# RMS norms of a decoder layer: the constant in a padded column, and one small step on another engine

## The chip, the cores and the metric

The kernel runs on one core of a Trainium2 chip, as one launch. The metric is the device time of that launch in microseconds (us). Instruction streams of five engines run side by side and meet only at semaphores: TensorE (PE, with its weight loads PEld), VectorE (DVE), ScalarE (ACT), GpSimd (POOL) and SyncE (SP, here used to issue DMAs). Each engine takes its own instructions in order.

## What is computed

One layer of a decoder over 1024 rows (tokens) of 1024 columns, in float32. With the sizes of this case (`DEPTH = 1`) the mixer is the pooling one:

```python
def rms_norm(x, g):
    xf = x.astype(jnp.float32)
    y = xf * lax.rsqrt(jnp.mean(xf * xf, axis=-1, keepdims=True) + EPS)
    return (y * g.astype(jnp.float32)).astype(x.dtype)
...
    h = rms_norm(x, norm_mix_g[layer])
    y = pool_mixer(h, pool_w[j], pool_b[j], pool_scale[j])
    x = x + y.astype(x.dtype)
    f = conv_ffn(rms_norm(x, norm_ffn_g[layer]), ffn_w_in[layer], ...)
    x = x + f.astype(x.dtype)
```

`pool_mixer` takes causal window means of 2, 4, 8 and 16 rows in four groups of columns, subtracts the row itself and multiplies each group by a 256x256 matrix. `conv_ffn` multiplies by a 1024x5632 matrix, convolves over three rows, gates with silu and multiplies by a 2816x1024 matrix. Nearly all the arithmetic lies in these last two products.

## The kernel before, in words

**Stages.** The 1024 rows are eight tiles of 128 rows, x0 to x7. In the first stage (to about 65 us of the profile) each tile goes through the mixer: its norm "a" (Square with a sum over the row on ACT, then a square root, then the factor on DVE), a band matrix scaled by that factor (`bandr`, `mixer_norm`), window sums by PE (`psd`), a copy to SBUF by ACT (`dh`), the 256x256 products and the bias by PE (`psy`), and the residual sum by DVE, which overwrites the tile (`mixer_out`, L267). Then follow the second norm "b", its application (`n2`, `ffn_norm`, L279), and eight transposes by PE (`pst`, `ffn_operand`). The rows that a window needs from the tile before come from a ninth tile, `x_edge`, whose own norm "e" scales `edge_band`, and whose window sums are `ps_edges`. In the second stage the 1024x5632 product runs by a Strassen-like scheme of seven products on operands that are each split in two (high part copied by ACT, L76 or L313; remainder by DVE, L77 or L314): banks X, Y, Z, L374. The third stage is the 2816x1024 product (L731), built likewise.

**The norm's arithmetic.** With m the sum of squares plus D*EPS and s the square root of m, one over s is wanted, but s comes from a table and is a little off. The kernel forms q = s*s + m and uses s divided by q (a factor two is folded into the weights). `rstd_of` (L154 to L163) issues, for each norm: on ACT Square with a sum (L157, one ACTIVATE and one read of the accumulator) and Sqrt with the constant as bias (L158); on DVE an addition of the constant to the sum (L159), s*s + m (L161) and a reciprocal (L162). There are 17 of them: a0 to a7, e, b0 to b7.

**What sets the order.** A scheduler lays each engine's instructions out by data dependences and by the hints `issue_after`, which hold an instruction back in the order until another has been placed. The tiles x2 to x6 lie in the pool `pre`, x0, x1 and x7 in the ring of seven buffers `hl` that later holds the split operands. SP's queue carries in order the loads of x, the stores of the new x (L268), the loads of the first weights (L322) and of one block of them (`S3`, L341). POOL's queue adds weight blocks to each other by accumulating DMAs (L336); their results are the operands S1, S2 and S4 of the second product.

Of the kernel before, what the change touches and what calls it, by code (L numbers as in the profile page):

```python
# [7 lines left out]
F32 = mybir.dt.float32  # L8
F32R = mybir.dt.float32r
BF16 = mybir.dt.bfloat16  # L10
AF = mybir.ActivationFunctionType
ALU = mybir.AluOpType
PSUM = bass.MemoryType.PSUM

P = 128
S = 1024
D = 1024
# [8 lines left out]
EPS = 1e-6  # L26
# [15 lines left out]
XBUFS = 5  # L42
# [6 lines left out]
def trunk_kernel(ctx: ExitStack, tc: tile.TileContext, x, consts, par, rows, pool_w, w_in, w_out, out):  # L49
    nc = tc.nc  # L50
# [6 lines left out]
    hls = ctx.enter_context(tc.tile_pool(name="hls", bufs=1))  # L57
# [4 lines left out]
    pp = pre.enter_context(tc.tile_pool(name="pre", bufs=1))  # L62
# [17 lines left out]
        return t  # L80


    xs = {}

    def load_x(j):
        if j < 2 or j >= 2 + XBUFS:
            xs[j] = hls.tile([P, D], F32, tag="hl", name=f"x{j}", bufs=7)
        else:
            xs[j] = pp.tile([P, D], F32, tag="x", name=f"x{j}", bufs=XBUFS)
        nc.sync.dma_start(xs[j], x[j * P : (j + 1) * P, :])  # L90

    cst = pp.tile([P, BD], F32, tag="cst", name="cst")
# [7 lines left out]
    scale = rows_raw[:, 0, :GRP]  # L100
# [33 lines left out]

    keep_warm(7)
    load_x(0)
    nc.sync.dma_start(cst[:, :E0], consts[:, :E0])
    load_x(1)
    nc.sync.dma_start(par_sb[:, GM:], par[:, GM:])
    nc.sync.dma_start(cst[:, E0:], consts[:, E0:])  # L140
    for g in range(0, NG, 2):
        nc.sync.dma_start(wp_raw[:, 2 * g : 2 * g + 4, :], pool_w[g : g + 2].rearrange("g (k p) d -> p (g k) d", p=P))
    load_x(2)

    nc.sync.dma_start(x_edge, x.rearrange("(j r) d -> r j d", r=P)[P - HALO :, :, :])
# [4 lines left out]
    ident = cst[:, ID:]  # L150

    marks = {}

    def rstd_of(src, name):  # L154
        junk = pp.tile([P, D], BF16, tag="junk", name=f"junk_{name}")
        st = pp.tile([P, 4], F32, tag="st", name=f"st_{name}", bufs=8)
        nc.scalar.activation(junk, src, AF.Square, accum_out=st[:, 0:1])  # L157
        marks[name] = nc.scalar.activation(st[:, 1:2], st[:, 0:1], AF.Sqrt, bias=eps_t).ins  # L158
        nc.vector.tensor_scalar(st[:, 0:1], st[:, 0:1], D * EPS, None, op0=ALU.add)  # L159

        nc.vector.scalar_tensor_tensor(st[:, 3:4], st[:, 1:2], st[:, 1:2], st[:, 0:1], op0=ALU.mult, op1=ALU.add)  # L161
        nc.vector.reciprocal(st[:, 2:3], st[:, 3:4])  # L162
        return st[:, 1:2], st[:, 2:3]  # L163
# [4 lines left out]
    bands, stats = {}, {}  # L168
# [84 lines left out]
    n2s = {}  # L253
    x1_dram = dram.tile([S, D], F32, tag="x1_dram", name="x1_dram")

    def mixer_out(j, stats=True):
        dh = ds.pop(j)
        ps = bank2(f"psy{j}")
        for c in range(NK):
            o = ps[:, c // 2 * GRP : (c // 2 + 1) * GRP]  # L260
            nc.tensor.matmul(o, dh[:, c, :], wps[:, c, :], start=c % 4 == 0, stop=False, skip_group_check=True)  # L261
        for h in range(2):
            cols = slice(h * NH, (h + 1) * NH)
            m = nc.tensor.matmul(ps[:, cols], ones, bias_hl[:, cols], start=False, stop=True, skip_group_check=True)  # L264
        marks[f"psy{j}"] = m.ins
        x1 = n2s[j] = xs.pop(j)
        marks[j] = nc.vector.tensor_tensor(x1, ps, x1, ALU.add).ins  # L267
        nc.sync.dma_start(x1_dram[j * P : (j + 1) * P, :], x1)  # L268
        if stats:
            mixer_out_stats(j)  # L270

    def mixer_out_stats(j):
        n2s[j] = (n2s[j], rstd_of(n2s[j], f"b{j}"))

    def ffn_norm(j):
        x1, r = n2s[j]
# [177 lines left out]

    def stat(j):
        if j in xs and j not in stats:
            stats[j] = rstd_of(xs[j], f"a{j}")

    scale_b = scale_rows()
    stat(0)  # L460
    mixer_norm(0)
    with tc.issue_after(marks["band0"]):
        nc.vector.tensor_tensor(b8, b8, rows8[:, 0, :], ALU.mult)
        stat(1)
# [12 lines left out]
    with tc.issue_after(marks["gain"]), tc.issue_after(marks["wps"]):  # L477
        stat(2)
        mixer_norm(2)
# [14 lines left out]
    with tc.issue_after(marks["band3"]), tc.issue_after(marks["edges"]):  # L494
        mixer_out_stats(0)
# [66 lines left out]
    def take(name):  # L562
# [15 lines left out]
    src = {  # L578
        "A11": lambda f: g_dram[f][:, s0], "A21": lambda f: g_dram[f][:, s1],
        "A12": lambda f: g_dram[f + NP2][:, s0], "A22": lambda f: g_dram[f + NP2][:, s1],  # L580
        "B11": lambda f: w_out[f * P : (f + 1) * P, s0], "B12": lambda f: w_out[f * P : (f + 1) * P, s1],
        "B21": lambda f: w_out[(f + NP2) * P : (f + NP2 + 1) * P, s0],
        "B22": lambda f: w_out[(f + NP2) * P : (f + NP2 + 1) * P, s1],
    }
# [91 lines left out]
    for k in range(-SLOOK, len(oevents)):  # L676
        p, f = oevents[k + SLOOK] if k + SLOOK < len(oevents) else (None, 0)
# [8 lines left out]
        with tc.issue_after(lasts[-1]) if lasts else nullcontext():  # L686
# [12 lines left out]
            p, f = oevents[k]  # L699
# [9 lines left out]
        if f == 0 and opens:  # L709
            for i in range(4):  # L710
                tag = ("XXYY" if set_ == "X" else "YZZZ")[i]
# [14 lines left out]
        for i, g, c, bank in steps:  # L726
            a, b = oops[p, g]
# [88 lines left out]
```

## Time and profile before

| | |
|---|---|
| time of the runs before, us | 701.71, 700.93, 700.96 (median 700.96) |
| profiled execution: span from first to last instruction, us | 699.1 |
| busy in that span | PE 692.5, PEld 575.8, DVE 597.9, ACT 343.0, POOL 13.3 us |
| granted TensorE clock | 1.000 |

The profile is of one execution, of which the span is known and not a time of its own; the timed runs are 1.8 to 2.6 us above that span. A row of the timeline gives start, duration, engine, source line, operation, output and input with their shapes, and in brackets how long the engine had been idle before and what ended that. A row of the chain of waits gives start, length and work of one piece of the path that ended last. A busy PE is not PE at its peak: matmuls overlap, and recorded ends lie some 0.2 us late.

### The profile page before, as it was taken

To read this page: it belongs to the slowest core of one execution; us is meant where nothing else is said; L and a number is where in the kernel's file an instruction comes from. 1 tells how busy PE (TensorE), PEld (TensorE's weight loads), DVE (VectorE), ACT (ScalarE), POOL (GpSimd) and SP (SyncE) were. 2 spreads that over 40 slices of the span, in tenths; PEclk is the share of its full clock that TensorE was granted. 3 is DMA by queue.
4 is the path that set the end of the run, shared out by engine and by line. 5 is a ranking of instruction groups with operands and counts; after the bars stand their busy time and mean duration, and the time that the engine had idled before them with its cause. 6 is when DMAs were issued, how large, how long until landed. Compare 5 with 4: busy or idle time off the path is not lost.

```text
span 699.1 us, 8512 instructions
## 1 busy us (share of the span) xinstructions
PE 692.5 (99%) x3164; PEld 575.8 (82%) x3164; DVE 597.9 (86%) x883; ACT 343.0 (49%) x515; POOL 13.3 (2%) x33
## 2 busy tenths in 40 slices
PE   9999999999999999999999999999999999999998
PEld 7898778888888888888888888888888888888886
DVE  4798999999888888888888888876887988999985
ACT  6686645554454454444454444444454344444431
POOL 3020000000000000000000000000000000000000
PEclk9999999999999999999999999999999999999999
DMA  8964112322212112222222212229989700122231
GB/s 279 304 170 121 61 60 91 120 91 91 90 64 89 68 57 86 91 91 90 91 90 91 91 69 82 97 87 350 326 301 339 269 22 0 61 90 89 63 106 61
DMA packets 32562, 85.49 MB, mean 122 GB/s; under 512 B 3692, under 2 KB 5384, under 8 KB 29704
## 3 DMA queue, kind: packets, MB, share of 16 engines
q1 hardware_dynamic: 31328, 82.83, 33.3%
q0 software_dynamic: 1184, 2.11, 1.7%
q8 instruction: 25, 0.41, 0.2%
q14 instruction: 17, 0.14, 0.1%
q10 hardware_dynamic: 8, 0.00, 0.0%
HBM read 62.89 MB, written 19.92 MB: 118 GB/s over the span
## 4 chain that ended last, share of the span: by engine, by line
PE 98%; DVE 1%; ACT 0%; issue 0%; POOL 0%; DVEq 0%; POOLq 0%
PE oP L731 30%; PE Y L374 26%; PE Z L374 17%; PE X L374 16%; PE psy L261 4%; PE psd L179 2%; PE pst L294 1%; PE psy L264 1%; DVE n2f L325 0%; PE idle_ps L133 0%; PE ps_scale L199 0%; DVE T L314 0%; PE ps_edges L179 0%; PE ps_gain L225 0%; DVE n L279 0%; DVE S4s L77 0%
## 5 line engine op out<-in xcount | busy, mean ns | idle before, releaser
L731 PE MATMUL oP<-oBP,oAP 128*128 128x512 f32 (+1 forms) x924 | 208.9, 388 | 0.0
L731 PEld LDWEIGHTS oP<-oBP,oAP 128*128 128x128 f32 x924 | 172.9, 188 | 36.0 <-DVE oBP L77 0.3
L374 PE MATMUL Z<-T,S1s 128*128 128x512 f32 x264 | 64.0, 390 | 1.5 <-ACT T L313 1.2
L374 PE MATMUL X<-B,A11s 128*128 128x512 f32 x264 | 64.3, 390 | 0.0
L374 PE MATMUL Y<-T,S2s 128*128 128x512 f32 x264 | 64.0, 390 | 0.0
L374 PE MATMUL X<-B,A12s 128*128 128x512 f32 x264 | 63.5, 390 | 0.0
L374 PE MATMUL Y<-T,S3s 128*128 128x512 f32 x264 | 63.4, 389 | 0.0
L374 PE MATMUL Y<-T,A22s 128*128 128x512 f32 x264 | 63.4, 389 | 0.0
L374 PE MATMUL Z<-B,S4s 128*128 128x512 f32 x264 | 63.2, 389 | 0.0
L374 PEld LDWEIGHTS Z<-T,S1s 128*128 128x128 f32 x264 | 49.3, 188 | 12.6 <-ACT T L313 1.7
L374 PEld LDWEIGHTS Y<-T,S2s 128*128 128x128 f32 x264 | 49.4, 188 | 10.8 <-ACT S2s L76 0.4
L374 PEld LDWEIGHTS Y<-T,S3s 128*128 128x128 f32 x264 | 49.5, 188 | 10.3
L374 PEld LDWEIGHTS Z<-B,S4s 128*128 128x128 f32 x264 | 49.6, 188 | 10.3
L374 PEld LDWEIGHTS Y<-T,A22s 128*128 128x128 f32 x264 | 49.6, 188 | 10.3
L374 PEld LDWEIGHTS X<-B,A12s 128*128 128x128 f32 x264 | 49.5, 188 | 10.2
L374 PEld LDWEIGHTS X<-B,A11s 128*128 128x128 f32 x264 | 49.4, 188 | 10.2
L76 ACT ACTIVATE oBP<-blk 128x512 fp32r<-128x512 f32 x53 | 33.5, 633 | 49.1 <-PE oP L731 32.2
L77 DVE TENSOR_TENSOR oBP<-blk,oBP 128x512 fp32r<-128x512 f32 x53 | 36.6, 691 | 13.0 <-ACT oBP L76 13.0
L432 ACT ACTIVATE gate<-gate 128x1024 f32<-128x1024 f32 x22 | 23.4, 1061 | 44.8 <-DVE gate L423 44.5
L76 ACT ACTIVATE oAP<-blk 128x512 fp32r<-128x512 f32 x55 | 34.1, 621 | 18.9 <-DVE blk L325 15.9
L328 DVE TENSOR_TENSOR win<-win 128x512 f32<-128x512 f32 x60 | 41.2, 687 | 1.1
L77 DVE TENSOR_TENSOR oAP<-blk,oAP 128x512 fp32r<-128x512 f32 x55 | 37.7, 685 | 2.6 <-ACT oAP L76 2.6
(129 smaller groups left out, 940.7 us busy)
## 6 DMA issues: line engine op xcount, KB each, us to landing
win<-in_w_in_dram SPq DMA_DIRECT2D x22, 1024.0 KB, 4.8
g_dram<-val SPq DMA_DIRECT2D x22, 512.0 KB, 2.6
blk<-g_dram SPq DMA_DIRECT2D x33, 256.0 KB, 5.3
blk<-in_w_out_dram SPq DMA_DIRECT2D x31, 256.0 KB, 5.9
A12s<-g_dram SPq DMA_DIRECT2D x22, 256.0 KB, 4.9
B21s<-in_w_out_dram SPq DMA_DIRECT2D x22, 256.0 KB, 2.6
x<-in_x_dram SPq DMA_DIRECT2D x8, 512.0 KB, 5.5
x_dram<-x SPq DMA_DIRECT2D x8, 512.0 KB, 2.8
```

Source lines behind the costliest of these rows:

```text
L76: nc.scalar.activation(t[:, 0, :], src, AF.Copy)
L77: m = nc.vector.tensor_tensor(t[:, 1, :], src, t[:, 0, :].bitcast(F32), ALU.subtract)
L179: m = nc.tensor.matmul(ps[:, c * P : (c + 1) * P], src[:, c * P : (c + 1) * P], weights[:, c // 2, :], start=True, stop=True)
L261: nc.tensor.matmul(o, dh[:, c, :], wps[:, c, :], start=c % 4 == 0, stop=False, skip_group_check=True)
L264: m = nc.tensor.matmul(ps[:, cols], ones, bias_hl[:, cols], start=False, stop=True, skip_group_check=True)
L294: nc.tensor.transpose(ps[:, c * P : (c + 1) * P], n2[:, c * P : (c + 1) * P], ident)
L328: nc.vector.tensor_tensor(out, a, b, ALU.add)
L374: nc.tensor.matmul(bank, a[:, i, ks], b[:, l, k, :], start=opens and m == 0, stop=m == 11, skip_group_check=not opens)
L432: nc.scalar.activation(gate, gate, AF.Silu)
L731: nc.tensor.matmul(bank, a[:, u, i * P : (i + 1) * P], b[:, v, c], start=opens and first, stop=g == NP2 - 1 and m == 2, skip_group_check=n ...
```

## The change

Each x tile becomes one column wider (1025), and a memset on DVE writes the square root of D*EPS into that column when its load is placed. For the a and b norms, Square runs over 1025 columns, so that its sum is m already: Sqrt has no bias, and the addition L159 is gone. For all of these but a0 and a1, s*s + m is an Identity on ACT with s as scale and m as bias; DVE keeps the reciprocal alone. The norm "e" of `x_edge` keeps the old form. The tile written by DVE's residual sum is the first 1024 columns, so that norm b finds the constant in place.

```diff
+        nc.vector.memset(padded[j][:, D:], (D * EPS) ** 0.5)
+        xs[j] = padded[j][:, :D]
         nc.sync.dma_start(xs[j], x[j * P : (j + 1) * P, :])
...
+    def rstd_padded(src, name, on_act):
+        junk = pp.tile([P, D + 1], BF16, tag="junk", name=f"junk_{name}")
+        st = pp.tile([P, 4], F32, tag="st", name=f"st_{name}", bufs=8)
+        ms, root, q, inv = (st[:, i : i + 1] for i in range(4))
+        nc.scalar.activation(junk, src, AF.Square, accum_out=ms)
+        marks[name] = nc.scalar.activation(root, ms, AF.Sqrt).ins
+        if on_act:
+            marks[name] = nc.scalar.activation(q, root, AF.Identity, bias=ms, scale=root).ins
+        else:
+            nc.vector.scalar_tensor_tensor(q, root, root, ms, op0=ALU.mult, op1=ALU.add)
+        nc.vector.reciprocal(inv, q)
+        return root, inv
...
-        n2s[j] = (n2s[j], rstd_of(n2s[j], f"b{j}"))
+        n2s[j] = (n2s[j], rstd_padded(padded.pop(j), f"b{j}", True))
...
-            stats[j] = rstd_of(xs[j], f"a{j}")
+            stats[j] = rstd_padded(padded[j], f"a{j}", j > 1)
```

The scheduler moves other work with it. Three places matter later. The first is ACT at tile 2 and the edge tile, before:

```order
L157 ACTIVATE junk_a2_250,st_a2_251<-x2_145 128x1024
L158 ACTIVATE st_a2_251<-st_a2_251,eps_t_89 128x1
L246 ACTIVATE dh1_268<-psd1_259 128x1024
L157 ACTIVATE junk_e_270,st_e_271<-x_edge_83 128x1024
L158 ACTIVATE st_e_271<-st_e_271,eps_t_89 128x1
```

and the same place now:

```order
L160 ACTIVATE junk_a2_256,st_a2_257<-x2_147 128x1025
L161 ACTIVATE st_a2_257<-st_a2_257 128x1
L163 ACTIVATE st_a2_257<-st_a2_257 128x1
L261 ACTIVATE dh1_273<-psd1_264 128x1024
L172 ACTIVATE junk_e_275,st_e_276<-x_edge_83 128x1024
L173 ACTIVATE st_e_276<-st_e_276,eps_t_89 128x1
```

One instruction more (the Identity, L163) now stands ahead of the copy dh1 and of the edge tile's Square. The second place is DVE at the last norm, b7, before:

```order
L159 TENSOR_SCALAR st_b7_695<-st_b7_695 128x1
L314 TENSOR_TENSOR T1_155<-n2f_153,T1_155 128x4x128
L161 SCALAR_TENSOR_TENSOR st_b7_695<-st_b7_695 128x1
L325 TENSOR_TENSOR n2f_153<-n2f_153,pst6_719 128x4x128
L162 RECIPROCAL st_b7_695<-st_b7_695 128x1
L325 TENSOR_TENSOR n2f_153<-n2f_153,pst6_719 128x4x128
L278 TENSOR_TENSOR st_b7_695<-st_b7_695 128x1
L325 TENSOR_TENSOR n2f_153<-n2f_153 128x4x128
L279 SCALAR_TENSOR_TENSOR n2_7_701<-x7_229,st_b7_695,gain_b_248 128x1024
```

and now:

```order
L329 TENSOR_TENSOR T1_158<-n2f_156,T1_158 128x4x128
L166 RECIPROCAL st_b7_688<-st_b7_688 128x1
L340 TENSOR_TENSOR n2f_156<-n2f_156,pst6_711 128x4x128
L293 TENSOR_TENSOR st_b7_688<-st_b7_688 128x1
L340 TENSOR_TENSOR n2f_156<-n2f_156,pst6_711 128x4x128
L294 SCALAR_TENSOR_TENSOR n2_7_693<-x7_234,st_b7_688,gain_b_254 128x1024
```

Two small instructions are gone, and n2_7 has moved up past one subtraction (L325 before, L340 now). The third place is DVE just after, where it makes the last part of the operand T1 (with S1s, the operand of the product Z), before:

```order
L77 TENSOR_TENSOR S4s_0_799<-win0_421,S4s_0_799 128x512
L77 TENSOR_TENSOR S4s_1_802<-win1_546,S4s_1_802 128x512
L325 TENSOR_TENSOR n2f_153<-n2f_153,pst7_749 128x4x128 x2
L325 TENSOR_TENSOR n2f_153<-n2f_153 128x4x128
L77 TENSOR_TENSOR S2s_0_805<-win0_421,S2s_0_805 128x512
L314 TENSOR_TENSOR T1_155<-n2f_153,T1_155 128x4x128
```

and now:

```order
L77 TENSOR_TENSOR S4s_0_791<-win0_420,S4s_0_791 128x512
L340 TENSOR_TENSOR n2f_156<-n2f_156,pst7_741 128x4x128 x2
L340 TENSOR_TENSOR n2f_156<-n2f_156 128x4x128
L329 TENSOR_TENSOR T1_158<-n2f_156,T1_158 128x4x128
L77 TENSOR_TENSOR S4s_1_794<-win1_541,S4s_1_794 128x512
L77 TENSOR_TENSOR S2s_0_797<-win0_420,S2s_0_797 128x512
```

T1's last part has moved ahead of S4s_1 and S2s_0. From there to S2s_2, the next operand that PE waits for, both orders hold the same instructions on DVE. On SP, the load of S3_0 now stands behind the store of the new x1 instead of ahead of it.

More of the change, by code (lines that the diff above doesn't have):

```diff
@@ L80, in split @@
         return t
-    xs = {}
+    xs, padded = {}, {}
     def load_x(j):
         if j < 2 or j >= 2 + XBUFS:
-            xs[j] = hls.tile([P, D], F32, tag="hl", name=f"x{j}", bufs=7)
+            padded[j] = hls.tile([P, D + 1], F32, tag="hl", name=f"x{j}", bufs=7)
         else:
-            xs[j] = pp.tile([P, D], F32, tag="x", name=f"x{j}", bufs=XBUFS)
+            padded[j] = pp.tile([P, D + 1], F32, tag="x", name=f"x{j}", bufs=XBUFS)
+        nc.vector.memset(padded[j][:, D:], (D * EPS) ** 0.5)
+        xs[j] = padded[j][:, :D]
         nc.sync.dma_start(xs[j], x[j * P : (j + 1) * P, :])
```

## Prediction

> **What bounds the kernel now.** The page first: the span and each engine's share.
>
> ```profile
> span 699.1 us, 8512 instructions
> PE 692.5 (99%) x3164; PEld 575.8 (82%) x3164; DVE 597.9 (86%) x883; ACT 343.0 (49%) x515; POOL 13.3 (2%) x33
> ```
>
> PE is the bound as a whole, so the change is worth what it takes from PE's waits, or adds to them. The norms lie in the first 66 us. The windows view, cut where the kernel's behaviour changes (columns: window, its length, busy time of PE, PEld, DVE, ACT, POOL, then the granted clock, DMA share and GB/s), and PE's own waits in the first 64 us:
>
> ```profile
> 20.50:64.50 44.00, 43.74 (x260) 39.46 (x261) 35.74 (x81) 34.15 (x62) 6.94 (x8) 1.00 0.70 196
> 64.50:76.70 12.20, 10.99 (x61) 8.93 (x58) 12.10 (x22) 9.24 (x17) 0.00 (x0) 1.00 0.11 43
> 76.70:103.10 26.40, 26.14 (x113) 20.77 (x113) 26.25 (x32) 11.95 (x16) 0.00 (x0) 1.00 0.22 80
> 103.10:130.00 26.90, 26.90 (x120) 22.26 (x120) 26.90 (x36) 16.47 (x22) 0.00 (x0) 1.00 0.21 79
> ```
> ```profile
> PE idle_ps L133 <- POOL idle L104: 1.4, 1, 1.4
> PE psy L261 <- DVE dh L251: 0.4, 1, 0.4
> ```
>
> Up to 64.5 us PE waits twice: at the very start, and 0.4 us for the edge rows. DVE has 8 us of idle time there, so freeing it gains nothing there. From 64.5 us on DVE is full (12.10 of 12.20, 26.25 of 26.40, 26.90 of 26.90), and PE waits for it. Rows of the timeline (start, duration, engine, line) give the places:
>
> ```profile
> 76.73 0.73 PE L374 MATMUL Z<-T,S1s 128*128 128x512 f32 x2 [1.24 <-ACT T L313]
> 77.69 5.28 PE L374 MATMUL Z<-T,S1s 128*128 128x512 f32 x22 [0.23 <-DVE T L314]
> ...
> 102.31 0.68 DVE L77 TENSOR_TENSOR S2s<-win,S2s 128x512 fp32r<-128x512 f32 x1
> ...
> 103.06 0.48 PE L374 MATMUL Y<-T,S2s 128*128 128x512 f32 x1
> ```
>
> PE loses 1.24 + 0.23 us at Z, and then stops again at 103.06, 0.07 us after DVE has finished S2s_2 (102.31 + 0.68 = 102.99). After that there is no wait up to 130 us. So two numbers decide: when PE gets through the edge rows (20 us), and when DVE gets to S2s_2 (102 us).
>
> **The change part by part.** *Memsets.* A memset of this shape takes 0.06 us, and three of them stand on DVE ahead of the first norm, where DVE waits 4.38 us:
>
> ```profile
> 1.15 0.06 DVE L107 MEMSET eps_t<- 128x1 f32 x1
> ...
> 5.73 0.15 DVE L159 TENSOR_SCALAR st_a<-st_a 128x1 f32<-128x1 f32 x1 [4.38 <-ACT st_a L158]
> ```
>
> The other five stand between the first of the `wps` products and the bias remainder, and take 0.3 us at 10 us; the PE waits above show that PE asks nothing of DVE in these 20 us before the edge rows. Cost 0. One column more on 1024 is a thousandth of a Square: 0. Norms a0 and a1 get shorter by the addition, but PE had no wait for them: 0.
>
> *The edge rows.* Norm a2 gets its Identity on ACT, and the edge tile's norm stands behind it. The rows, with one bias-free Sqrt (L110) for its price:
>
> ```profile
> 3.12 0.20 ACT L110 ACTIVATE warm<-eps_t 128x1 f32<-128x1 f32 x1
> ```
> ```profile
> 14.18 0.19 ACT L157 ACTIVATION_READ_ACCUMULATOR junk_a<-x 128x1 f32 x1
> 14.40 0.29 ACT L158 ACTIVATE st_a<-st_a,eps_t 128x1 f32<-128x1 f32 x1
> 14.60 1.00 ACT L246 ACTIVATE dh<-psd 128x1024 f32<-128x1024 f32 x1
> 15.51 1.05 ACT L157 ACTIVATE junk_e<-x_edge 128x1024 bf16<-128x1024 f32 x1
> ```
> ```profile
> 17.65 0.55 DVE L166 TENSOR_SCALAR edge_band<-cst,st_e 128x512 f32<-128x512 bf16 x1
> ...
> 18.32 1.87 PEld L179 LDWEIGHTS ps_edges<-edge_band,x_edge 128*128 128x128 f32 x16
> ```
> ```profile
> 16.80 1.78 PE psd L179 x16
> 18.59 1.80 PE ps_edges L179 x16
> ...
> 20.41 0.30 DVE dh L251
> ...
> 20.76 3.72 PE psy L261 x16
> ```
>
> Sqrt without a bias column takes 0.20 us, with one 0.29: 0.09 for a column. Identity with two is not in this trace in so small a shape; I take 0.20 + 2 x 0.09 = 0.38, and the next instruction 0.09 before its end, as dh1 at 14.60 started 0.09 before the end of Sqrt (14.69). Identity needs Sqrt's result, and ACT's own result costs 0.03 (14.18 + 0.19 to 14.40). So: Sqrt 14.40 to 14.60, Identity from 14.63, dh1 at 14.92 instead of 14.60: 0.32 us late. What follows has no gap: dh1, the edge Square, its Sqrt, DVE's three small steps and edge_band all move by 0.32, and edge_band ends at 18.52 instead of 18.20. PE wants it at 18.32 for the first weight load, right behind psd2 (the chain has 16.80 + 1.78 and then 18.59, without a gap). At least 0.05 us pass from DVE's end to PE (T's end 76.96 + 0.68 to Z at 77.69, by the next rows), so PE is held until 18.57 to 18.64: **+0.28 us**. The wait for the edge sum (20.41) and psy1 behind it follow ps_edges and move along. Bounds: 0 (Identity overlaps Sqrt and costs its 0.20 spacing less the column's 0.09, and a margin of 0.07 lies at PE) to 0.41 (nothing overlaps). Nothing later gives this back: psy7, with which the full stretch of DVE begins, hangs on PE alone.
>
> *DVE's full stretch.* Of the 16 norms, fourteen lose two DVE instructions, but only b7 lies in the full stretch:
>
> ```profile
> 67.62 0.63 ACT L313 ACTIVATE T<-n2f 128x512 fp32r<-128x512 f32 x1
> ```
> ```profile
> 68.09 0.14 DVE L159 TENSOR_SCALAR st_b<-st_b 128x1 f32<-128x1 f32 x1
> 68.29 0.69 DVE L314 TENSOR_TENSOR T<-n2f,T 128x512 fp32r<-128x512 f32 x1
> 68.90 0.21 DVE L161 SCALAR_TENSOR_TENSOR st_b<-st_b 128x1 f32<-128x1 f32 x1
> 69.03 0.68 DVE L325 TENSOR_TENSOR n2f<-n2f,pst 128x512 f32<-128x512 f32 x1
> ...
> 76.96 0.68 DVE L314 TENSOR_TENSOR T<-n2f,T 128x512 fp32r<-128x512 f32 x1
> ...
> 91.17 0.69 DVE L403 TENSOR_TENSOR q<-Y,q 128x512 f32<-128x512 f32 x1
> ```
>
> L159 takes 0.20 of DVE's time (68.09 to 68.29) and L161 0.13 (68.90 to 69.03), 0.33 together. But T at 68.29 came 0.04 after ACT's end (68.25), so of the 0.20 only the 0.09 counts by which ACT's Sqrt ahead of that T gets shorter: 0.22. Z itself will start much earlier, since T's last part has moved ahead of S4s_1 and S2s_0: at 0.6 each, as T above (68.29 to 68.90), they and the 0.2 come to about 1.4 us, of PE's 1.24 + 0.23. This does not last. From T to S2s_2 DVE has the same work to do in either order, so S2s_2 comes earlier only by what DVE no longer does and by idle time that it loses. Of idle time there is 0.10 + 0.15 us by the windows; the 0.15 I put down to q at 91.17, which waits for PE's Y0. Z being earlier, it could shrink; but one of T3's two parts now stands behind q instead of ahead of it, so DVE comes to q 1.1 us earlier and waits about as long as before. Gain at S2s_2: 0.22 less up to 0.1; I take **-0.15 us**. Bounds: -0.58 (0.33 and all the 0.25 of idle time) to +0.2 (r_1 and q, by my sum, come to PE's results with less than 0.1 us to spare, and each could wait 0.1 more).
>
> The rule of the Trainium skill for such a profile (Perfetto Trace Analysis, Identifying the Most-Contended Engine) is to take work from the engine with the highest occupancy first; in these rows that is DVE. By that rule the norms' 0.33 would come off the end in full, and the sum would be -0.05 instead of +0.13; the trace agrees with the rule only for b7, since DVE is not the fullest engine at the other norms.
>
> *SP and POOL.* The load of S3_0 stands behind x1's store, at most 7 us later than before (20.21 and 27.27); POOL's sums follow it:
>
> ```profile
> 20.21 0.94 SPq L341 DMA_DIRECT2D S<-in_w_in_dram  x1
> 27.27 0.33 SPq L268 DMA_DIRECT2D x_dram<-x  x1
> ```
> ```profile
> 28.48 0.89 POOL L336 DMA_DIRECT2D S<-win  x1 [21.32 <-DMA S<-in_w_in_dram]
> ...
> 55.88 1.16 ACT L76 ACTIVATE S1s<-win 128x512 fp32r<-128x512 f32 x2
> ```
>
> The first reader of a sum is ACT at 55.88, 27 us after POOL's first issue: cost 0 unless the sums come over 10 us late.
>
> Sum against the profiled execution: 699.1 + 0.28 - 0.15 = 699.23. The runs' median is 700.96, 1.86 above that span; I keep this distance: **701.1**.
>
> **The rivals.** *The start of Z carries through.* If something else frees DVE between T and S2s_2, PE keeps the 1.24 + 0.23: 700.96 + 0.28 - 1.47 = 699.8. For it: T does move ahead. Against it: 26.25 us busy of 26.40, the same instructions, and PE's stop at 103.06. Chance 0.10.
>
> *ScalarE becomes the bound* (slower). At tiles 3 to 5 ACT is almost full, and PE takes back a PSUM bank just after ACT has copied it out:
>
> ```profile
> 37.00:50.00 13.00, 13.00 (x85) 11.95 (x84) 12.09 (x29) 12.01 (x21) 4.34 (x5) 1.00 0.72 167
> ```
> ```profile
> 36.75 1.01 ACT L246 ACTIVATE dh<-psd 128x1024 f32<-128x1024 f32 x1
> ...
> 37.92 0.50 PE L179 MATMUL psd<-bandr,x 128*128 128x128 f32 x3
> ```
>
> ACT has 0.99 us left of 13. Each norm adds 0.29 - 0.09 = 0.20 there, and four Identities come to 0.8. dh4 ends at 37.76, 0.16 before psd5. If the added steps make these copies later than that margin, each of six tiles costs PE 0.2 to 0.4: +1.2 to +2.4, about 702.7. Against it: both norms of a tile also start earlier, since DVE's residual sum no longer queues behind three small steps, and laid along the new order with these durations dh4 ends 0.1 late while PE is 0.28 late. The Trainium skill (ScalarE: Activation LUTs, Rules for kernel authors) gives adds and multiplies to VectorE and not to ScalarE; this rival is that rule at work, and the edge rows are a small case of it. Chance 0.13.
>
> *The change does nothing where it counts* (the edge norm had room, and T's wait for ACT eats b7's gain): 700.96, inside my range. Other things, as sums by POOL that come late: 0.05.
>
> **How the numbers follow.** My own case, with 0.72, reaches from 700.96 + 0 - 0.58 = 700.4 to 700.96 + 0.41 + 0.2 = 701.6. To hold 8 in 10 I go out to 699.9, almost to the first rival, and to 702.2, where the second begins. A measurement can tell about 0.2%, 1.4 us, from no change: under 699.56 lie the first rival's lower part and half of the rest (0.07), above 702.36 most of the second and the other half (0.13), and 0.80 remain.
>
> **What would show it.** Right: ps_edges starts at about 18.85 in the chain, Z near 76.6, and PE stops once more at S2s_2, near 103.2. Wrong: ps_edges at 18.6 (my price of Identity); S2s_2 on DVE before 101.5 (first rival); waits of PE for ACT between 30 and 60 us, or X's first product later than 58.3 (second rival).

## The result, and the profile after

The change makes the kernel slower by 2.3%: 717.19 us (median of 5, 716.56 to 717.30) against 701.09 for the kernel before (median of 5, 700.93 to 701.71), ratio 1.0226, 95% interval 1.0215 to 1.0238. The forecast of 701.1 missed by 16 us. The profiled execution after has a span of 715.4 us, 16.3 more than the 699.1 of before. The page's first lines of the kernel after, to be set beside the two at the head of the prediction:

```profile
span 715.4 us, 8510 instructions
PE 708.4 (99%) x3164; PEld 575.0 (80%) x3164; DVE 596.0 (83%) x861; ACT 345.3 (48%) x529; POOL 13.4 (2%) x33
```

PE is busy 15.9 us longer with as many instructions, while DVE and ACT change by some 2 us. So PE does not wait longer: its work takes longer. First, the stretch that the prediction was about. The waits of PE in the whole kernel after:

```profile
PE idle_ps L135 <- POOL idle L106: 1.4, 1, 1.4
PE ps_edges L194 <- ACT st_a L161: 0.7, 1, 0.7
PE Y L389 <- ACT val L436: 0.6, 1, 0.6
PE psd L194 <- DVE bandr L181: 0.4, 1, 0.4
PE psy L276 <- DVE dh L266: 0.4, 1, 0.4
PE Z L389 <- DVE T L329: 0.2, 1, 0.2
```

And the rows of the timeline after that answer to the prediction's, first on ACT and DVE, then on PE and DVE:

```profile
13.58 1.06 ACT L160 ACTIVATE junk_a<-x 128x1025 bf16<-128x1025 f32 x1 [1.83 <-DMA x<-in_x_dram]
...
14.99 0.39 ACT L163 ACTIVATE st_a<-st_a 128x1 f32<-128x1 f32 x1
15.29 1.01 ACT L261 ACTIVATE dh<-psd 128x1024 f32<-128x1024 f32 x1
...
18.33 0.55 DVE L181 TENSOR_SCALAR edge_band<-cst,st_e 128x512 f32<-128x512 bf16 x1
```
```profile
18.98 2.02 PE L194 MATMUL ps_edges<-edge_band,x_edge 128*128 128x128 f32 x16 [0.69 <-ACT st_a L161]
...
76.98 3.27 PE L389 MATMUL Z<-T,S1s 128*128 128x512 f32 x13 [0.25 <-DVE T L329]
...
102.97 0.68 DVE L77 TENSOR_TENSOR S2s<-win,S2s 128x512 fp32r<-128x512 f32 x1
...
103.73 2.33 PE L389 MATMUL Y<-T,S2s 128*128 128x512 f32 x9
```

Here things went much as forecast. The Identity lasts 0.39 us and holds the copy dh1 back by 0.30. PE's 0.69 us at the edge rows are a wait for `edge_band`, which DVE ends at 18.88, and not for the Sqrt that the profile names: in every run here in which PE waits at this place, its first matmul starts 0.10 us after the end of `edge_band`. Z's 1.24 us wait for ACT is gone, but 0.57 us come back as a wait ahead of Y from A22s, at 99.61 us, for ACT's `val`, which had itself waited 1.81 us for DVE. And DVE, still full, brings PE to a stop again at S2s_2, at 103.73 (before: 103.06). Two thirds of a microsecond is all that is lost in the first 104 us. The rest comes later, where no norm is left. The windows view of PE alone in the second and third product (window, length, busy time and number of matmuls, granted clock, DMA share, GB/s), of before and then of after:

```profile
160.00:480.00 320.00, 320.00 (x1413) 1.00 0.25 91
490.00:690.00 200.00, 200.00 (x884) 1.00 0.42 144
```
```profile
160.00:480.00 320.00, 320.00 (x1377) 1.00 0.23 82
490.00:690.00 200.00, 200.00 (x860) 1.00 0.47 161
```

PE is busy without a gap in both, at the full granted clock; but in 320 us it gets through 1377 matmuls, not 1413: 232.4 ns each, not 226.5. With 2772 such matmuls (7 groups of 264 and 924), 5.9 ns more on each is 16.4 us, as much as the whole loss. (Two half-wide matmuls are counted as one in the 924.) Two groups of the second product before, and then one round of it after, in the timeline of PE (the start of the next row less the start of a row is what a group of 12 takes):

```profile
311.70 2.88 PE L374 MATMUL Y<-T,A22s 128*128 128x512 f32 x12
314.42 2.88 PE L374 MATMUL X<-B,A11s 128*128 128x512 f32 x12
```
```profile
301.14 2.97 PE L389 MATMUL X<-B,A11s 128*128 128x512 f32 x12
303.96 2.97 PE L389 MATMUL Y<-T,S2s 128*128 128x512 f32 x12
306.76 2.96 PE L389 MATMUL Z<-T,S1s 128*128 128x512 f32 x12
309.56 2.92 PE L389 MATMUL X<-B,A12s 128*128 128x512 f32 x12
312.32 2.96 PE L389 MATMUL Y<-T,S3s 128*128 128x512 f32 x12
315.12 2.95 PE L389 MATMUL Z<-B,S4s 128*128 128x512 f32 x12
317.90 2.96 PE L389 MATMUL Y<-T,A22s 128*128 128x512 f32 x12
320.70 1.57 PE L389 MATMUL X<-B,A11s 128*128 128x512 f32 x6
```

Six groups take 2.78 to 2.82 us and one, X from A12s, 2.76; before, all take 2.72. The round takes 19.56 us instead of 7 times 2.72 = 19.04. Every round shows the same groups with the same times, so this is no jitter; and the DMA moves no more than before in the first window (82 against 91 GB/s), so it is not traffic there. Along the chain of waits, the second product from S2s_2 (103.22 before, 103.90 after) to the start of the third (485.94, 496.84) takes 382.7 and 392.9 us, and the third 208.7 and 214.2: 10.2 + 5.5, with the first 0.7 about the 16.3 of the span.

What can make a matmul longer whose instruction has not changed? The diff has one more effect than its words say: `hls.tile([P, D + 1], ..., tag="hl", bufs=7)`. x0, x1 and x7 lie in the ring that later holds the split operands, all seven buffers have the size of the largest tile, and the allocation rounds sizes up to 32 bytes. A buffer grew from 4096 to 4128 bytes in each partition, so the operands moved. In the allocation of the built programs, in bytes past a multiple of 4096 (after: in 19 or 20 of the 22 rounds; in the first rounds the ring deals its buffers out in another order):

```
stationary operands (ring hl)           A11s  S2s   S1s   A12s  S3s   S4s   A22s
  before                                 928   928   928   928   928   928   928
  after                                 1088  1056   992   928   960  1024  1120
moving operands, in the same order       B11   T2    T1    B21   T3    B22   T4
  before                                 928   928   928   928   928   928   928
  after                                  928  1152   928   928  1152  1152  1152
```

A stationary operand is the one that is loaded into PE as weights; the moving one streams through it. Only A12s and B21 still start alike, and theirs is the least slowed group. In the third product both operands come from the ring; before, all 77 pairs start alike, after, all are 32 to 96 bytes apart.

### The profile page after: what moved, and what is told of

Read it like the earlier page. It is cut to its first block, busy times and chain, and to the rows that moved or that the text cites. A ratio compares the mean times of both kernels' runs of the same rounds, so it can differ in the third digit from the quotient of the medians.

```text
span 715.4 us, 8510 instructions
## 1 busy us (share of the span) xinstructions
PE 708.4 (99%) x3164; PEld 575.0 (80%) x3164; DVE 596.0 (83%) x861; ACT 345.3 (48%) x529; POOL 13.4 (2%) x33
## 4 chain that ended last, share of the span: by engine, by line
PE 94%; DVE 2%; DMA 2%; ACT 1%; issue 0%; DVEq 0%
PE oP L746 30%; PE Y L389 25%; PE Z L389 17%; PE X L389 16%; PE psy L276 3%; DMA x<-in_x_dram 2%; PE psd L194 1%; DVE n2f L340 1%; DVE T L329 1%; PE pst L309 1%; PE psy L279 0%; ACT junk_a L160 0%; DVE n2f L343 0%; PE ps_edges L194 0%; DVE S1s L77 0%
## 5 line engine op out<-in xcount | busy, mean ns | idle before, releaser
L746 PE MATMUL oP<-oBP,oAP 128*128 128x512 f32 (+1 forms) x924 | 214.4, 394 | 0.0
L389 PE MATMUL X<-B,A11s 128*128 128x512 f32 x264 | 66.2, 397 | 0.0
L389 PE MATMUL Z<-T,S1s 128*128 128x512 f32 x264 | 65.6, 396 | 0.2 <-DVE T L329 0.2
L389 PE MATMUL Y<-T,A22s 128*128 128x512 f32 x264 | 65.2, 395 | 0.6 <-ACT val L436 0.6
L389 PE MATMUL Y<-T,S2s 128*128 128x512 f32 x264 | 65.7, 396 | 0.0
L389 PE MATMUL Y<-T,S3s 128*128 128x512 f32 x264 | 65.0, 395 | 0.0
L389 PE MATMUL Z<-B,S4s 128*128 128x512 f32 x264 | 64.7, 394 | 0.0
L77 DVE TENSOR_TENSOR oBP<-blk,oBP 128x512 fp32r<-128x512 f32 x53 | 36.7, 692 | 16.4 <-ACT oBP L76 15.4
L76 ACT ACTIVATE oAP<-blk 128x512 fp32r<-128x512 f32 x55 | 34.1, 621 | 19.5 <-DVE blk L340 15.9
```

Source lines behind the costliest of these rows:

```text
L76: nc.scalar.activation(t[:, 0, :], src, AF.Copy)
L77: m = nc.vector.tensor_tensor(t[:, 1, :], src, t[:, 0, :].bitcast(F32), ALU.subtract)
L389: nc.tensor.matmul(bank, a[:, i, ks], b[:, l, k, :], start=opens and m == 0, stop=m == 11, skip_group_check=not opens)
L746: nc.tensor.matmul(bank, a[:, u, i * P : (i + 1) * P], b[:, v, c], start=opens and first, stop=g == NP2 - 1 and m == 2, skip_group_check=n ...
```

## The experiments

Two theories were set against each other: that the places of the operands slow the matmuls, and, as rival, that the changed instructions do.

**The layout alone.** The kernel before, with longer buffers and nothing else:

```diff
-        return hls.tile([P, 2, NH], F32R, tag="hl", name=name, bufs=7)
+        return hls.tile([P, 2 * NH + 8], F32R, tag="hl", name=name, bufs=7)[:, : 2 * NH].rearrange("p (a b) -> p a b", a=2)
...
-            xs[j] = hls.tile([P, D], F32, tag="hl", name=f"x{j}", bufs=7)
+            xs[j] = hls.tile([P, D + 8], F32, tag="hl", name=f"x{j}", bufs=7)[:, :D]
```

> Before, with no changed instruction: only the seven buffers of the ring hl are 32 bytes longer, as the padded x0, x1 and x7 make them in the changed kernel, so that operand tiles lie at the same places in SBUF as there (A11s 1088, S2s 1056, S1s 992, A12s 928, S3s 960, S4s 1024, A22s 1120 and T2, T3, B22, T4 1152 bytes past a multiple of 4096; in before all of them at 928). Theory P (the places of the operands slow the matmuls): 717, 716 to 718, and 128x512 matmuls of the second product that start 230 to 235 ns apart on average, not 226.6. Rival I (the changed instructions, their waits and ScalarE's extra work slow it): 701, 700.3 to 701.8, and 226.6 ns.

Measured: 716.09 us (4 runs, 716.07 to 716.23), ratio 1.0210 (1.0194 to 1.0225). PE's windows:

```profile
160.00:480.00 320.00, 320.00 (x1378) 1.00 0.23 82
490.00:690.00 200.00, 200.00 (x862) 1.00 0.47 160
```

232.2 ns each, as in the kernel after: 14.8 of the 16.1 us come without one changed instruction. The rival is out as the main cause. The 1.3 us left between this kernel and the changed one can be placed along the chain of waits: 0.55 us lie ahead of S2s_2 (103.35 here, 103.90 in the changed kernel), 0.5 in the second product and 0.4 in the third. In these two products the operands are not paired quite alike (A11s and S1s have each other's buffers here, so A11s lies at 992 and S1s at 1088), and a round takes 19.53 us on average instead of 19.55.

**The change without the layout.** The new norms for the ten of x2 to x6, which lie in the pool `pre`; x0, x1 and x7 unpadded, with the old norm:

```diff
-            padded[j] = hls.tile([P, D + 1], F32, tag="hl", name=f"x{j}", bufs=7)
+            xs[j] = hls.tile([P, D], F32, tag="hl", name=f"x{j}", bufs=7)
...
-            stats[j] = rstd_padded(padded[j], f"a{j}", j > 1)
+            stats[j] = rstd_padded(padded[j], f"a{j}", j > 1) if j in padded else rstd_of(xs[j], f"a{j}")
...
```

> The change for the ten norms of x2 to x6 alone, which lie in another pool: every operand of the big products keeps its place of before; x0, x1, x7 keep the old norm. Theory P: 226.6 ns between matmuls everywhere, and a time that my forecast's terms give without the last norm's part: 701.1 + 0.3, so 700.6 to 702.0. Rival I: ten of the sixteen changed norms are still there, so at least half of the 16 us: 709 or more.

Measured: 701.80 us (11 runs) against 701.33, ratio 1.0004 (0.9996 to 1.0013), and 1414 matmuls in the first window. So the layout without the change brings the loss, and ten of the changed norms without the layout do not.

**One pool moved.** Is it the place of an operand by itself, or the distance between two? A gap of 224 bytes behind the ring moves T2, T3, B22 and T4 alone:

```diff
+    gap = ctx.enter_context(tc.tile_pool(name="gap", bufs=1))
+    nc.vector.memset(gap.tile([P, 56], F32, tag="gap", name="gap"), 0.0)
     work = ctx.enter_context(tc.tile_pool(name="work", bufs=1, side="right"))
```

> Before, with a gap of 224 bytes behind the ring hl: only T2, T3, B22, T4 move (928 to 1152 past a multiple of 4096); all stationary operands and B11, T1, B21 stay at 928. Theory P, form 'difference' (a matmul loses when its stationary and its moving operand start at different offsets): the groups with T2, T3, B22, T4 take 2.76 to 2.81 us and those with B11, T1, B21 2.72; 4 of 7 groups at about 0.076 more, 22 times, so 707 to 708.5; third product unchanged. Theory P, form 'single' (each operand has good and bad places by itself): the same four groups, or none, slow; stationary ones cannot differ. Rival I: 701.

Measured: 708.66 us (one run; before 701.33), just above the 707 to 708.5 of the form 'difference'. PE's timeline, one round:

```profile
301.98 2.96 PE L376 MATMUL Y<-T,S2s 128*128 128x512 f32 x12
304.78 2.91 PE L376 MATMUL Z<-T,S1s 128*128 128x512 f32 x12
307.53 2.88 PE L376 MATMUL X<-B,A12s 128*128 128x512 f32 x12
310.25 2.96 PE L376 MATMUL Y<-T,S3s 128*128 128x512 f32 x12
313.05 2.96 PE L376 MATMUL Z<-B,S4s 128*128 128x512 f32 x12
315.85 2.96 PE L376 MATMUL Y<-T,A22s 128*128 128x512 f32 x12
318.65 2.91 PE L376 MATMUL X<-B,A11s 128*128 128x512 f32 x12
321.39 0.86 PE L376 MATMUL Y<-T,S2s 128*128 128x512 f32 x3
```

The four groups with a moved operand take 2.80 us. Of the three others, A12s takes 2.72, but S1s and A11s, which follow a slow group, take 2.75 and 2.74: 25 ns more than the expectation had. The starts of the single matmuls show why (mean ns to the next start, by the matmul's number in its group, over 16 or 17 rounds):

```
                       1     2     3     4     5     6     7     8     9    10    11    12
one pool moved
  S2s, T2 (224 off)  234.2 235.0 231.7 235.0 231.6 235.0 231.6 235.0 231.7 235.0 231.6 235.0
  S1s, T1 (0)        230.0 235.8 228.3 232.5 230.8 226.7 226.7 226.6 226.7 226.7 226.6 226.7
  A12s, B21 (0)      226.7 226.6 226.7 226.7 226.6 226.7 226.7 226.6 226.7 226.7 226.6 226.7
layout alone
  A12s, B21 (0)      235.8 228.4 232.4 230.8 226.8 226.6 226.6 226.8 226.6 226.6 226.8 235.0
```

A group that comes after a slow one needs four or five matmuls to get back to 226.7. And with the layout alone the last matmul of A12s, whose own operands start alike, takes 235.0: what is different at that moment is that the weights of the next group (S3s, at 960) are loaded while B21 (928) streams (the first of these loads runs from 3 to 191 ns after that matmul's start). In the moved pool's kernel the next weights are at 928 as well, and the last takes 226.7. The third product, whose operands did not move, keeps its time, although the DMA moves as much in this window as in the changed kernel (159 GB/s against 161):

```profile
490.00:690.00 200.00, 200.00 (x884) 1.00 0.46 159
```

**All operands moved alike.** The same gap, of 32 bytes, ahead of all operand pools; everything starts at 960:

> Before, with a gap of 32 bytes ahead of all operand pools: all operands at 960 past a multiple of 4096, stationary and moving alike. Form 'difference': 701, 226.6 ns between matmuls. Form 'single' (928 is a good place and others are not): every group slow or changed, 705 to 720. Rival I: 701.

Measured: 701.40 us (one run; before 701.33), all groups 2.72 us. So 928 is not special: a difference between two operands is what costs. The kernel with the layout alone says the same of 960: that place costs nothing here, where both operands lie there, but there the matmul that streamed from 928 took 235.0 ns while weights at 960 were loaded. A rule by which single places are good or bad does not give that.

**Four distances in one kernel.** B22, T4, T3 and T2 start 16, 256, 512 and 768 bytes off the stationary ones, by longer buffers and a slice that begins later (`at` counts elements of 4 bytes; the buffers' own starts move by the rest):

```diff
...
+        t = pool.tile([P, 8 * NH + 48], F32R, tag="nop", name=name, bufs=7 - NOPS_A)
+        at = {"B22": 4, "T4": 16, "T3": 32, "T2": 48}[name]
+        return t[:, at : at + 8 * NH].rearrange("p (a b c) -> p a b c", a=2, b=4)
...
```

> Before, with the four operands of one pool moved by different amounts against the stationary ones (all still at 928 past a multiple of 4096): B22 by 16 bytes, T4 by 256, T3 by 512, T2 by 768; B11, T1, B21 unmoved. Theory 'difference modulo 512' (all slices of before already differ by multiples of 512, and cost nothing): T3 stays at 226.6 ns between matmuls; T2, T4 at 256 off cost as the 224 bytes did, 233 ns; B22 at 16 bytes slow too if the unit is 16 or smaller, else 226.6. Theory 'modulo 256': T2, T3 and T4 all at 226.6. Theory 'any difference costs, whatever its size' : T2, T3, T4 and B22 all at 231 to 234, and 708 to 709 us as with the 224 bytes. By the first with B22 slow: about 706 to 707.5; by the second: 701 to 703.5.

Measured: 703.39 us (one run; before 701.34). One round in the chain of waits:

```profile
302.43 2.72 PE Z L378 x12
305.15 2.72 PE X L378 x12
307.87 2.72 PE Y L378 x12
310.59 2.78 PE Z L378 x12
313.37 2.75 PE Y L378 x12
316.12 2.72 PE X L378 x12
318.84 2.72 PE Y L378 x12
```

In the order S1s, A12s, S3s, S4s, A22s, A11s, S2s: 512 and 768 bytes (the Y from S3s at 307.87, the Y from S2s at 318.84) cost nothing; 16 bytes (Z from S4s, 310.59) cost 0.06 us for the group. 256 bytes (A22s, 313.37) show 2.75, but by single matmuls it runs at 226.6 ns from the seventh on, so this is what the slow group ahead of it leaves. That is 'modulo 256', the second theory. Together with the table of the kernel after, where 32, 64, 96, 128, 160 and 192 bytes are all slow, every distance tried that is no multiple of 256 costs 0.06 to 0.09 us on 12 matmuls, and no multiple of 256 costs anything (the last kernel below has A11s and A22s 256 bytes off, and all its groups take 2.72).

**The whole change, minus the column in the ring.** What was the forecast's own sum worth? ScalarE adds the constant at x0, x1 and x7, whose tiles are not padded (norms a0 and a1 keep the old form):

```diff
+    def rstd_act(src, name):
...
+        marks[name] = nc.scalar.activation(root, ms, AF.Sqrt, bias=eps_t).ins
+        nc.scalar.activation(m, ms, AF.Identity, bias=eps_t)
+        marks[name] = nc.scalar.activation(q, root, AF.Identity, bias=m, scale=root).ins
+        nc.vector.reciprocal(inv, q)
...
```

> The whole change but for the way the constant gets in at x0, x1, x7, whose tiles stay 1024 columns: there ScalarE adds it in one more small Identity ahead of s*s+m (a0 and a1 keep the old norm). VectorE is left with the reciprocal for b0 to b7 and a2 to a7, and every operand lies as in before. It measures what my forecast summed, with the costs of layout taken out. My forecast's terms: ps_edges 0.3 to 0.6 later, Z's start 1 to 1.5 us ahead against X's, PE stopped again at S2s_2, so 700.8 to 701.8. The rival that Z's gain is kept: 699.6 to 700.4. ScalarE as the bound: 702 to 704.

Measured: 700.73 us (11 runs, 700.20 to 701.29) against 701.34, ratio 0.9992 (0.9983 to 1.0001): between the forecast's and the first rival's ranges, and not to be told from no change. The trace decides between them:

```profile
75.61 4.74 PE L400 MATMUL Z<-T,S1s 128*128 128x512 f32 x20
...
95.56 0.68 DVE L77 TENSOR_TENSOR A11s<-win,A11s 128x512 fp32r<-128x512 f32 x1
...
96.29 2.59 PE L400 MATMUL X<-B,A11s 128*128 128x512 f32 x10 [0.72 <-DVE A11s L77]
...
102.08 0.68 DVE L77 TENSOR_TENSOR S2s<-win,S2s 128x512 fp32r<-128x512 f32 x1
...
102.84 2.30 PE L400 MATMUL Y<-T,S2s 128*128 128x512 f32 x9
```

Z runs without a stop from 75.61; before, it had two matmuls at 76.73 and went on at 77.69, as if it had started at 77.24. Of these 1.6 us PE gives back 0.72 waiting for DVE at A11s, and stops once more at S2s_2, at 102.84 against 103.06: 0.2 us are kept. PE stops both times right behind DVE's end (96.24 and 102.76), so DVE is the limit of this stretch, as the forecast had it.

**Norm a2 left to VectorE.** As the last one, with `j > 2` in place of `j > 1`:

> As e8, with s*s+m of norm a2 left on VectorE, so that no small step more stands on ScalarE ahead of dh1 and the edge norm. If the edge rows are all that the rest of the change costs, PE's wait of 0.2 to 0.7 us at ps_edges goes and the time is 0.2 to 0.4 below e8, 700.5 to 701.3, and no more than 0.5 below before. If the delay is of the loads and not of that step, the same as e8.

Measured: 700.91 us (11 runs), ratio 0.9993 (0.9985 to 1.0002): no gain over the last kernel. In its trace the edge tile's products start 4.99 us after x2 is there (13.72 to 18.71), against 5.40 (13.17 to 18.57) with the Identity on ACT and 5.21 before (13.22 to 18.43, where PE was still at psd2). The end of `edge_band` on DVE is the cleaner mark, since it does not depend on when PE is free: it comes 5.30 or 5.31 us after x2 in the five runs with the Identity on ACT, 4.97 or 4.98 in the five with the old norm, and 4.88 here. So the changed norm a2 costs 0.33 us there, and leaving s*s + m to DVE gives back 0.42. In the time of the kernel it does not show: the moment at which x2 lands varies by more from run to run (12.46 to 13.72 over all runs here).

**The whole change with the ring repaired.** Three of the seven buffers, for x0, x1 and x7, get 256 bytes more and not 32; there is no room for seven. In a first form tiles were dealt to the two kinds of buffers by counting:

```diff
...
+        if ring.n % 7 < 3:
+            return hls.tile([P, D + 64], dtype, tag="hlx", name=name, bufs=3)[:, :width]
+        return hls.tile([P, D], dtype, tag="hl", name=name, bufs=4)
...
```

> The whole changed kernel, padded x0, x1, x7 and all; only the ring is repaired: its three buffers that hold x0, x1, x7 are 256 bytes longer instead of 32, the other four as before. Operands then lie at 928, 1184, 1440 and 1696 bytes past a multiple of 4096, all apart by multiples of 256. If the places of the operands are the whole loss and multiples of 256 cost nothing: 226.6 ns between matmuls everywhere and 700.2 to 701.6 us, as the change without the column in the ring. If multiples of 256 do cost something, or the changed instructions do: 703 or more. It is also the version that could beat both: below 700.2 it would by more than its intervals.

Measured: 707.07 us (5 runs) against 701.18, ratio 1.0082 (1.0068 to 1.0096), not the 700.2 to 701.6 expected. The matmuls are back at 1413 in the first window, but a new wait has come, in ACT's timeline:

```profile
37.88 0.62 ACT L84 ACTIVATE A11s<-win 128x512 fp32r<-128x512 f32 x1
43.18 0.63 ACT L84 ACTIVATE S1s<-win 128x512 fp32r<-128x512 f32 x1 [4.68 <-DMA win<-win]
43.72 0.58 ACT L336 ACTIVATE B<-pst 128x512 fp32r<-128x512 f32 x1
```

With buffers of two kinds the scheduler could place S1s earlier on ACT, ahead of the copies that PE needs; S1s waits for POOL's sums, and PE stood 4.1 us at the transposes. The second form deals the buffers out as the one ring did, and holds each high-part copy behind the one before:

```diff
...
+        with tc.issue_after(marks["hl"]) if "hl" in marks else nullcontext():
+            marks["hl"] = nc.scalar.activation(t[:, 0, :], src, AF.Copy).ins
...
```

> As e10, but the two kinds of buffers go to the tiles as the one ring dealt them out in the changed kernel, and each high-part copy is held behind the one before it, so that every engine carries exactly the changed kernel's instructions in its order. Only the places differ: multiples of 256 apart, not of 32. If the places are the whole loss of 16 us, and e10's 4.7 us of ScalarE waiting at S1s for POOL's sums came from its order: 226.6 ns, no such wait, and 700.2 to 701.5. If the wait stays (the places or the buffers bring it): 705 to 707. If something in the changed instructions costs besides: between, with 226.6 ns and another wait named by PE.

Measured: 701.15 us (11 runs, 700.56 to 702.39) against 701.60, ratio 0.9996 (0.9987 to 1.0005). PE's windows and its place at S2s_2:

```profile
160.00:480.00 320.00, 320.00 (x1414) 1.00 0.25 91
490.00:690.00 200.00, 200.00 (x883) 1.00 0.42 144
```
```profile
103.32 2.32 PE L400 MATMUL Y<-T,S2s 128*128 128x512 f32 x9
```

The same instructions in the same order as the slow kernel, only laid out otherwise, and all 16 us are gone. None of these versions beats the kernel before by more than its interval.

## Why the prediction was wrong

- **The step that failed** stands under "Memsets": "One column more on 1024 is a thousandth of a Square: 0." The column was costed as work and as nothing else. What it cost is place: seven buffers 32 bytes longer, operands up to 192 bytes off their partners, 5.9 ns on each of 2772 matmuls, 16 us. The layout alone gives 14.8 of it, and repairing the layout, with every instruction of the change in its place, takes all 16 away. Neither the sum nor any rival had a term after 104 us, and so no range could hold the result; the 0.05 for "other things" was the only room.
- **The edge rows, +0.28: right.** The Identity lasts 0.39 us with 0.30 to the next start, against 0.38 and 0.29 in the forecast, and counted from x2 `edge_band` ends 0.33 us later, against 0.32. ps_edges came at 18.98, not 18.85, because x2 landed 0.36 later in that execution: the first weight load waits until 18.95, 0.63 later than before, of which 0.27 are left without the landing.
- **DVE's full stretch, -0.15: right in kind.** Z moved ahead, the gain did not last, and PE stopped again at S2s_2. From the residual sum of x7, with which the stretch begins, to S2s_2 DVE takes 37.75 us before (64.56 to 102.31), 37.71 in the changed kernel (65.26 to 102.97) and 37.52 with the ring repaired (65.04 to 102.56): a gain of 0.04, and of 0.23 where the matmuls are not slowed. The difference between these two is DVE's waiting for PE's results at the sums r and q: 0.28 us in the changed kernel, 0.09 with the ring repaired (before: 0.15). In the kernel without the column in the ring the gain is 0.43, inside the bounds that I had set. S2s_2 on DVE at 102.97 (after) and 102.08 (without the column in the ring) is far from the 101.5 that the first rival needed.
- **ScalarE as the bound: did not happen.** PE waits for ACT nowhere between 30 and 60 us, and the one such wait later, 0.57 us at 99.61, goes back to DVE; X's first product starts at 58.25 in PE's timeline (57.59 before), within the 58.3 that I had set; of its 0.66 us, 0.55 were there at the edge rows. The rule of the Trainium skill (ScalarE: Activation LUTs, Rules for kernel authors) shows in the edge rows alone, as the 0.33 us there.
- **Memsets, a0 and a1, SP, POOL at 0: nothing speaks against it.** With the places repaired the whole change comes to 701.15 against 701.60, where the sum gave 0.13 more than before: within what can be told, no change, as the sum had it. The time alone could not tell the sum's +0.13 from its rivals near zero, but the two terms above were measured each by itself in the traces. So the sum was sound for the part of the kernel that it looked at.

## What to carry to other kernels

A tile that shares a ring or pool with operands of a product is part of their layout: before calling a wider tile free, see which tag it is in, what its buffers grow to, and what then moves. When matmuls lengthen with no wait and at the full clock, compare where their two operands start; of the distances tried here only multiples of 256 bytes cost nothing, and padding to such a multiple repaired it. And when one such edit is undone with more than one kind of buffer, the scheduler may reorder as well, so compare the order of the instructions before blaming the layout.

## What the runs showed of the hardware

- An fp32r matmul of 128x512 that follows others without a gap starts every 226.6 ns if the stationary and moving operands' starts in the partition differ by a multiple of 256 bytes (0, 256, 512, 768 were run), and every 227 to 241 ns, 231 to 234 on average over a group, if they don't (16, 32, 64, 96, 128, 160, 192, 224 were run). The pattern within a group is the same in every round, to within half a nanosecond. Of the distances tried none costs much less than another, though a group's figure also holds what its neighbours leave in it.
- The pair that matters seems to be the streaming operand and the weights that are loaded meanwhile: the last matmul of an aligned group takes 235.0 ns when the next group's weights lie 32 bytes off, and 226.7 when they don't. The Trainium skill (TensorE: Matmul & The Clock Gate, Step-by-step: what each phase is for) says that loading the next tile's weights takes no SBUF read bandwidth from the running matmul. That alone gives no reason why the places should matter; 232.4 against 226.5 ns here shows that they do for operands like these. How the two reads meet inside the chip, and why a slow group leaves four to six slow matmuls behind it, no run here shows. Nor was it tried whether matmuls with other types or shapes feel it.
- The Trainium skill (SBUF — State Buffer, Operand start alignment) lets a float32 operand start at any multiple of 4 bytes. That holds here; but starts 16 bytes off cost 2% (2.78 against 2.72 us for 12).
